# mLSTM state of a hybrid layer: the normalisers through the vector tile and one transpose, the sample state's load behind the last prompt chunk

## The chip, the cores and the metric

The kernel runs on one core of one Trainium2 chip. A core has a matrix engine (TensorE, PE in the profile; PEld is its weight load), a vector engine (VectorE, DVE), an activation engine (ScalarE, ACT), a general engine (GpSimd, POOL) and a queue engine (SyncE, SP) that issues DMA transfers. Each engine runs its own instructions in order; semaphores order them between engines. The metric is the device time of one execution in microseconds (us), the median of several runs.

## The reference

One layer of a streaming encoder, for 1024 prompt tokens without history and 64 sample tokens that continue a stored state. All arrays are float32, the model width is 1024.

```python
z = x @ w_in                      # conv GLU, q/k/v/o heads, gates, two merge gates
# branch A: GLU -> causal depthwise conv (31 taps) -> LayerNorm -> swish -> w_a_out
# branch B: mLSTM, 4 heads of 256; per chunk, with carried (C0, n0, m0):
num = einsum(s, v) + w_inter * einsum(q, C0)
den = sum(s)       + w_inter * einsum(q, n0)
h   = num / maximum(abs(den), exp(-m))
C1  = decay * C0 + einsum(w_end, k, v)
n1  = decay * n0 + einsum(w_end, k)
# head norm, output gate, w_b_out; merge; w_out; LayerNorm; feed-forward; LayerNorm
```

The matrix memory C is 256 x 256 for each head, the normaliser n has 256 numbers for each head. The prompt starts from zeros, the sample from `state_C`, `state_n` and `state_m`. Outputs are the tokens of both streams and, for both, the last 30 rows of the convolution, C, n and m.

## The kernel before

Activations stand feature-major in three chunks of tokens (384, 384 and 320). Every matrix product is done in three passes of rounded high and low parts (`mm3`, L325 to L330: high by high, low by high, high by low). A *unit* (L317) takes one piece of a weight matrix, 1024 x 128: for each of the three chunks of tokens it makes one product of 24 matmuls on PE, hands the result to its own `post` function, and calls `slot` (L119). The weight pieces are loaded two ahead on SP (`wload`, L1105) and split one ahead (`wsplit`, L1111), the high part on ACT, the low part on DVE (`split`, L332).

Beside the units run background generators, which `slot` moves on by hand: one step of the mLSTM of the current head, steps of the depthwise convolution, and one step of a third queue. The convolution's steps are paid from a credit: a slot adds 1.0 where an mLSTM step was done and 1.7 where none was, and each step of the convolution costs 1.0 (L119 to L124). What is left of a generator when a stage ends is drained at once (`drain`, L115). The order that a function writes down is not quite the order on an engine: the framework plans each engine's instructions anew within what their data allow, except where `pin` keeps them in program order. Each tile's buffer is reused when its last readers are done.

At the start, `start_x` (L174) loads and transposes x, then loads 31 rows of the convolution's weights and six rows of vectors into the tile `vp` (L181 to L184) and the convolution's cache into `cp` (L185). Eight transposes on PE turn `vp` into `vecs`, one column for each row and feature (L187 to L190), eight more turn `cp` into `cacheT`. The gates' small weights, bias and `state_m` are loaded next (L219 to L223), and a first product on PE with them is L238.

For each of the four heads, eight units make k, q, v and the output gate o; behind the first o unit the generator `mlstm(h)` (L419) is queued. It walks through nine chunks of 128 tokens: chunks 0 to 7 are the prompt, chunk 8 holds the 64 sample tokens. A chunk takes two steps:

- First half, L451 to L478: the scores k by q and the transposed k on PE, then on ACT and DVE the weighted scores `sm`, split into `smh` and `sml`, and the weighted k, `kwh` and `kwl`.
- Second half, L479 to L520: on PE the scores by v (the first is pinned and waits for `smh`), q by the carried state (`Ch`, `Cl`), and k by v for the new state; DVE makes the new C (L499) and the denominator's terms, POOL two small operations of the norm (L516, L517).

The state tile C is 128 x 2 x 258 with two buffers. Its column 256 holds n, because v has a column of ones there; column 257 is a pad. Its split (`csplit`, L433) makes `Ch` and `Cl`. In chunk 8 the carried state comes from memory: a C tile, its last columns zeroed on POOL (L455), the load of `state_C` (L456, 256 KB) and the load of `state_n` (L457, 1 KB: two numbers into column 256 of each partition), then the split. At the end of chunks 7 and 8 the new state is stored, C by L503 and its n column by L504. All these transfers are issued on SP, in the order L503, L504, L456, L457 at the turn from chunk 7 to chunk 8.

Behind the last head, `close_proj` (L615) drains the mLSTM and the convolution. Then `open_bra` (L651) splits the gated result into the next operand, and units of `w_b_out` begin while the first norm `ln_a` (L730) loads the convolution's output.

Of the kernel before, what the change touches and what calls it, by code (L numbers as in the profile page):

```python
# [9 lines left out]
F32 = mybir.dt.float32  # L10
F32R = mybir.dt.float32r
AF = mybir.ActivationFunctionType
# [9 lines left out]
P = 128  # L22
KT = D // P
NH = 4
HD = 256
CW = 31
CB = CW - 1
# [8 lines left out]
MASKED = -1.0e38  # L36
R_BDW, R_AG, R_AB, R_HN, R_G1, R_B1 = 31, 32, 33, 34, 35, 36
NV = 37

# [10 lines left out]
def hybrid_layer(ctx, tc, x_prompt, x_sample, cache_conv, state_C, state_n, state_m, w_in, b_gate,  # L50
# [3 lines left out]
    nc = tc.nc  # L54
    V, S, G, TE = nc.vector, nc.scalar, nc.gpsimd, nc.tensor
# [8 lines left out]
    const = pool("const")  # L64
# [4 lines left out]
    small = pool("small", 4)  # L69
# [14 lines left out]
    def mtile():  # L84
        return pools["psm"].tile([P, 512], F32, tag="m", name="m")
# [29 lines left out]
    def drain(kind):  # L115
        while step(kind):
            pass
# [7 lines left out]

# [1 line left out]
    ident = const.tile([P, P], F32, name="ident")  # L127
    make_identity(nc, ident)
    vecs = const.tile([P, KT, NV], F32, name="vecs")
# [10 lines left out]
    bgb = const.tile([P, 8], F32, name="bgb")  # L140
    smc = const.tile([P, 1], F32, name="smc")

    proj = ExitStack()

# [1 line left out]
    XH, XL = [], []  # L146
# [27 lines left out]
    def start_x():  # L174
        for i in range(3):
            trans_x(i, xt0[i])
            if i == 1:
                wsplit(0, True)
        for i in range(3, NT):
            trans_x(i, load_x(i))  # L180
        vp = xp.tile([NV, D], F32, tag="x", name="vp")  # L181
        nc.sync.dma_start(vp[0:CW, :], w_dw[0])
        for r, src in ((R_BDW, b_dw), (R_AG, ln_a_g), (R_AB, ln_a_b), (R_HN, hn_g), (R_G1, ln1_g), (R_B1, ln1_b)):
            nc.sync.dma_start(vp[r:r + 1, :], src[0:1, :])  # L184
        cp = xp.tile([CB, D], F32, tag="x", name="cp")  # L185
        nc.sync.dma_start(cp, cache_conv[0, 0])
        ps = mtile()  # L187
        for k in range(KT):
            TE.transpose(ps[:, k * NV:(k + 1) * NV], vp[:, k * P:(k + 1) * P], ident[:NV, :NV])
        V.tensor_copy(vecs, ps[:, :KT * NV].rearrange("p (k v) -> p k v", k=KT))  # L190
        ps = mtile()
        for k in range(KT):
            TE.transpose(ps[:, k * CB:(k + 1) * CB], cp[:, k * P:(k + 1) * P], ident[:CB, :CB])
        V.tensor_copy(cacheT, ps[:, :KT * CB].rearrange("p (k v) -> p k v", k=KT))

    N(start_x)

# [1 line left out]
    def gates():  # L199
# [106 lines left out]

# [1 line left out]
    early, later = [], []  # L308
# [38 lines left out]

# [1 line left out]
    G32 = []  # L349
# [69 lines left out]
    def mlstm(h):  # L419
        ml = pools["ml"]  # L420
        kf, qf, vh, vl, dt = HT["k"], HT["q"], HT["vh"], HT["vl"], HT["dt"]
        W = HD + 2
# [24 lines left out]

        C = Ch = Cl = back = None
        nxt = prep(0)
        for c in range(NT):  # L450
            n, o = tile_len(c), c * P  # L451
            qs, ks = nxt
            if c == 8:
                C = ml.tile([P, 2, W], F32, tag="C", name="C", bufs=2)
                G.memset(C[:, :, HD + 1:], 0.0)  # L455
                nc.sync.dma_start(C[:, :, :HD], state_C[0, 0, h].rearrange("(j p) v -> p j v", p=P))  # L456
                nc.sync.dma_start(C[:, :, HD:HD + 1], state_n[0, 0, h].rearrange("(j p o) -> p j o", p=P, o=1))  # L457
                Ch, Cl = csplit(C)
            pS = mtile()
            for j in range(2):  # L460
                a = TE.matmul(pS[:, :2 * P], ks[:, j, 0, :], qs[:, j].rearrange("p e t -> p (e t)"), start=j == 0, stop=False)
# [38 lines left out]
            C = Cn  # L500
            if c >= 7:
                Cd, nd = (C_prompt, n_prompt) if c == 7 else (C_sample, n_sample)
                nc.sync.dma_start(Cd[0, 0, h].rearrange("(j p) v -> p j v", p=P), C[:, :, :HD])  # L503
                nc.sync.dma_start(nd[0, 0, h].rearrange("(j p o) -> p j o", p=P, o=1), C[:, :, HD:HD + 1])  # L504
            else:
                Ch, Cl = csplit(C)
# [14 lines left out]
            back = (c, n, isb)  # L521
# [93 lines left out]
    def close_proj():  # L615
        drain("mlstm")
        drain("conv")
        proj.close()

    N(close_proj)  # L620

# [1 line left out]
    def set_operand(srcs, pad=False):  # L623
# [22 lines left out]

# [1 line left out]
    A32, MB = [], []  # L648
# [117 lines left out]

# [1 line left out]
    wos = ExitStack()  # L768
# [27 lines left out]

# [1 line left out]
    X1H, X1L, Y2 = [], [], []  # L798
# [48 lines left out]

# [1 line left out]
    stage[0] = 1  # L849
# [160 lines left out]

# [1 line left out]
    HID = {}  # L1012
# [86 lines left out]

# [1 line left out]
    pieces = [j for j in jobs if j[0] is not None]  # L1101
# [70 lines left out]
```

## Time and profile before

| | us |
|---|---|
| median of 3 runs (lowest, highest) | 2013.27 (2013.09, 2013.63) |
| span of the profiled execution | 2012.8 |
| PE busy | 1943.4 (97% of the span) |
| DVE busy | 1426.8 (71%) |
| ACT busy | 648.7 (32%) |
| POOL busy | 126.3 (6%) |

The profile is of one execution. Its span runs from the first to the last instruction; the runs' median is of other executions and lies 0.5 us above it. The mean granted clock of PE is 0.984 of full speed. The chain that ended last, followed back from the end, is 80% PE, 11% DVE, 4% DMA, 2% waiting for nothing that is shown, 2% ACT and 1% POOL.

How to read the rows that follow. A row of the timeline has the start and the length in us, the engine, the line, the operation, output<-inputs and shape; in brackets stands how long the engine was idle before it and who ended that. A row of the waits has the waiting instruction, whom it waited for, the total in us, the number of times and the longest. A row of the windows has the stretch, its length, the busy time and instructions of PE, PEld, DVE, ACT and POOL, the granted clock of PE, the share of the DMA engines and GB/s. A row of the chain has the start, the length and what it was. A row of the groups has the busy time, the mean in ns of one, and the idle time before them.

### The profile page before, as it was taken

What the parts mean: (1) busy time and instruction counts of PE and PEld (TensorE: products, weight loads), DVE (VectorE), ACT (ScalarE), POOL (GpSimd) and SP (SyncE); (2) the same over time, 40 slices, a digit from 0 to 9 for tenths busy, and PEclk for the clock granted to TensorE, in tenths of its full rate; (3) what the DMA queues carried; (4) which work ended last, traced back from release to release, by engine and by line L of the source; (5) the groups of instructions that cost most, each with busy time, mean ns of one, the idle gap of its engine ahead of it and who ended that gap; (6) DMA issues with size and microseconds to landing.
All of it is one profiled execution on the core that took longest, in us unless ns stands there. A gap on an engine that the chain in (4) does not pass through costs nothing.

```text
span 2012.8 us, 30485 instructions
## 1 busy us (share of the span) xinstructions
PE 1943.4 (97%) x12395; PEld 1917.8 (95%) x12395; DVE 1426.8 (71%) x2717; ACT 648.7 (32%) x1209; POOL 126.3 (6%) x220
## 2 busy tenths in 40 slices
PE   8999899998999899989999998999999999999996
PEld 7999899998999899989999998999999999999995
DVE  4957776786678677868885557877686858677647
ACT  4323222333233323323342204524233332414232
POOL 1112210001000100000000000000000000000005
PEclk9999999999999999989999999999999999999998
DMA  4122321122112221225325310111111111111212
GB/s 148 44 78 67 85 70 43 54 67 47 56 41 63 62 63 37 64 66 172 116 82 154 116 40 21 32 53 43 53 42 54 43 43 53 43 53 43 74 42 79
DMA packets 174974, 131.06 MB, mean 65 GB/s; under 512 B 11518, under 2 KB 169694, under 8 KB 174833
## 3 DMA queue, kind: packets, MB, share of 16 engines
q1 hardware_dynamic: 174833, 129.11, 21.8%
q8 instruction: 97, 1.59, 0.3%
q14 instruction: 44, 0.36, 0.1%
HBM read 104.39 MB, written 24.63 MB: 64 GB/s over the span
## 4 chain that ended last, share of the span: by engine, by line
PE 80%; DVE 11%; DMA 4%; issue 2%; ACT 2%; POOL 1%; SPq 0%; POOLq 0%; ACTq 0%; DVEq 0%
PE g L326 25%; PE g L329 25%; PE g L330 25%; DMA C<-in_state_n_dram 2%; DVE s L668 2%; DVE acc L563 1%; PE m L326 1%; PE m L330 1%; PE m L329 1%; DVE o L1091 1%; DVE wl L337 1%; DVE ln L640 0%; DVE a L689 0%; DVE y L689 0%; DVE C L499 0%
## 5 line engine op out<-in xcount | busy, mean ns | idle before, releaser
L326 PE MATMUL g<-xh,wh 128*128 128x384 f32 (+1 forms) x1920 | 636.0, 331 | 0.0
L329 PE MATMUL g<-xl,wh 128*128 128x384 f32 (+1 forms) x1920 | 630.1, 328 | 0.0
L330 PE MATMUL g<-xh,wl 128*128 128x384 f32 (+1 forms) x1920 | 629.6, 328 | 0.0
L326 PEld LDWEIGHTS g<-xh,wh 128*128 128x128 f32 x1920 | 363.1, 189 | 0.4 <-ACT xh L334 0.2
L329 PEld LDWEIGHTS g<-xl,wh 128*128 128x128 f32 x1920 | 363.0, 189 | 0.3
L330 PEld LDWEIGHTS g<-xh,wl 128*128 128x128 f32 x1920 | 362.6, 189 | 0.1
L563 DVE SCALAR_TENSOR_TENSOR acc<-glu,vecs,acc 128x1118 f32<-128x1118 f32 x240 | 332.8, 1387 | 3.9
L334 ACT ACTIVATE wh<-wr 128x1024 fp32r<-128x1024 f32 (+1 forms) x168 | 166.1, 989 | 429.1 <-PE g L329 356.0
L337 DVE TENSOR_TENSOR wl<-wr,wh 128x1024 fp32r<-128x1024 f32 (+1 forms) x168 | 191.4, 1139 | 106.8 <-ACT wh L334 104.2
L326 PE MATMUL g<-x1h,wh 128*128 128x384 f32 (+1 forms) x768 | 253.1, 330 | 0.0
L329 PE MATMUL g<-x1l,wh 128*128 128x384 f32 (+1 forms) x768 | 252.8, 329 | 0.0
L330 PE MATMUL g<-x1h,wl 128*128 128x384 f32 (+1 forms) x768 | 252.6, 329 | 0.0
L329 PE MATMUL g<-hvl,wh 128*128 128x272 f32 x784 | 223.5, 288 | 0.0
L330 PE MATMUL g<-hvh,wl 128*128 128x272 f32 x784 | 221.5, 288 | 0.0
L326 PE MATMUL g<-hvh,wh 128*128 128x272 f32 x784 | 221.1, 289 | 0.1
L967 DVE TENSOR_TENSOR y<-g,y 128x272 f32<-128x272 f32 (+1 forms) x540 | 157.3, 341 | 26.8 <-PE g L330 25.1
L326 PEld LDWEIGHTS g<-hvh,wh 128*128 128x128 f32 x784 | 145.9, 189 | 1.7 <-DVE y L967 1.4
L329 PEld LDWEIGHTS g<-hvl,wh 128*128 128x128 f32 x784 | 147.4, 188 | 0.1
L330 PEld LDWEIGHTS g<-hvh,wl 128*128 128x128 f32 x784 | 146.4, 188 | 0.0
L330 PEld LDWEIGHTS g<-x1h,wl 128*128 128x128 f32 x768 | 144.8, 188 | 0.0
L329 PEld LDWEIGHTS g<-x1l,wh 128*128 128x128 f32 x768 | 144.7, 188 | 0.1
L326 PEld LDWEIGHTS g<-x1h,wh 128*128 128x128 f32 x768 | 144.5, 188 | 0.1
(267 smaller groups left out, 2440.9 us busy)
## 6 DMA issues: line engine op xcount, KB each, us to landing
wr<-in_w_in_dram SPq DMA_DIRECT2D x64, 512.0 KB
wr<-in_w_ff_dram SPq DMA_DIRECT2D x64, 512.0 KB
x<-in_x_prompt_dram SPq DMA_DIRECT2D x8, 512.0 KB
dwT<-acc SPq DMA_DIRECT2D x8, 512.0 KB
wr<-in_w_b_out_dram SPq DMA_DIRECT2D x8, 512.0 KB
wr<-in_w_a_out_dram SPq DMA_DIRECT2D x8, 512.0 KB
wr<-in_w_out_dram SPq DMA_DIRECT2D x8, 512.0 KB
out_dram<-o SPq DMA_DIRECT2D x16, 256.0 KB
```

The lines of the kernel that those rows point to most:

```text
L326: first = TE.matmul(out, lh, rh, start=start, stop=False, skip_group_check=more)
L329: TE.matmul(out, lh, rl, start=False, stop=False, skip_group_check=more)
L330: TE.matmul(out, ll, rh, start=False, stop=stop, skip_group_check=more)
L334: a = S.activation(hi, src, AF.Copy)
L337: V.tensor_tensor(lo, src, hi.bitcast(F32), ALU.subtract)
L563: V.scalar_tensor_tensor(acc, glu[:, j:j + AC], vecs[:, c, j:j + 1], acc, ALU.mult, ALU.add))
L668: V.tensor_reduce(out[:, :n], t[:, :, :n].rearrange("p k t -> p t k"), AX.X, ALU.add)
L967: V.tensor_tensor(y, ps[:, pslc], y, ALU.add)
L1091: V.tensor_tensor(o[:n, hs], o[:n, hs], pools["g2"][:n, hs], ALU.mult)
```

## The change

`state_n` comes in as one more row of `vp` (1024 numbers, one DMA of 4 KB), so that it stands as one more column of `vecs`. The new state tile for chunk 8, `C0`, is made at the end of chunk 7's second half: the load of `state_C` is issued there, ahead of the store of C, and POOL zeroes the last columns and copies n's column from `vecs`. Chunk 8 begins with one more `yield` and then splits `C0`. The stores of n's column are replaced by a copy on POOL into a small tile `nout`; after the last head one transpose on PE, one copy on ACT and two stores, of eight rows of 128 numbers each, send all of it out. Comment lines that were also changed are left out.

```diff
-R_BDW, R_AG, R_AB, R_HN, R_G1, R_B1 = 31, 32, 33, 34, 35, 36
-NV = 37
+R_BDW, R_AG, R_AB, R_HN, R_G1, R_B1, R_SN = 31, 32, 33, 34, 35, 36, 37
+NV = 38
...
     smc = const.tile([P, 1], F32, name="smc")
+    nout = const.tile([P, 2, KT], F32, name="nout")
...
             nc.sync.dma_start(vp[r:r + 1, :], src[0:1, :])
+        nc.sync.dma_start(vp[R_SN:R_SN + 1, :], state_n[0, 0].rearrange("h k -> (h k)")[None, :])
         cp = xp.tile([CB, D], F32, tag="x", name="cp")
...
-        C = Ch = Cl = back = None
+        C = Ch = Cl = back = C0 = None
...
             if c == 8:
-                C = ml.tile([P, 2, W], F32, tag="C", name="C", bufs=2)
-                G.memset(C[:, :, HD + 1:], 0.0)
-                nc.sync.dma_start(C[:, :, :HD], state_C[0, 0, h].rearrange("(j p) v -> p j v", p=P))
-                nc.sync.dma_start(C[:, :, HD:HD + 1], state_n[0, 0, h].rearrange("(j p o) -> p j o", p=P, o=1))
+                yield
+                C = C0
                 Ch, Cl = csplit(C)
...
             if c >= 7:
-                Cd, nd = (C_prompt, n_prompt) if c == 7 else (C_sample, n_sample)
-                nc.sync.dma_start(Cd[0, 0, h].rearrange("(j p) v -> p j v", p=P), C[:, :, :HD])
-                nc.sync.dma_start(nd[0, 0, h].rearrange("(j p o) -> p j o", p=P, o=1), C[:, :, HD:HD + 1])
+                if c == 7:
+                    C0 = ml.tile([P, 2, W], F32, tag="C", name="C", bufs=2)
+                    nc.sync.dma_start(C0[:, :, :HD], state_C[0, 0, h].rearrange("(j p) v -> p j v", p=P))
+                    G.memset(C0[:, :, HD + 1:], 0.0)
+                    G.tensor_copy(C0[:, :, HD:HD + 1], vecs[:, 2 * h:2 * h + 2, R_SN:R_SN + 1])
+                nc.sync.dma_start((C_prompt if c == 7 else C_sample)[0, 0, h].rearrange("(j p) v -> p j v", p=P), C[:, :, :HD])
+                G.tensor_copy(nout[:, c - 7, 2 * h:2 * h + 2, None], C[:, :, HD:HD + 1])
...
     def close_proj():
         drain("mlstm")
+        ps = mtile()
+        TE.transpose(ps[:2 * KT, :P], nout.rearrange("p a k -> p (a k)"), ident)
+        nt = small.tile([CB, 2 * P], F32, tag="cb", name="nt", bufs=1)
+        S.activation(nt[:2 * KT, :P], ps[:2 * KT, :P], AF.Copy)
+        for a, dst in ((0, n_prompt), (1, n_sample)):
+            nc.sync.dma_start(dst[0, 0].rearrange("h (j p) -> (h j) p", p=P), nt[a * KT:(a + 1) * KT, :P])
         drain("conv")
         proj.close()
```

## The prediction, made before the changed kernel had run

> **What bounds the kernel now.** I read the page first, then the totals of waits, then the timeline around the longest of them. The page says that the matrix engine (PE) is the bound nearly everywhere, and that one DMA stands on the chain that ended last:
>
> ```profile
> span 2012.8 us, 30485 instructions
> PE 1943.4 (97%) x12395; PEld 1917.8 (95%) x12395; DVE 1426.8 (71%) x2717; ACT 648.7 (32%) x1209; POOL 126.3 (6%) x220
> ...
> PE g L326 25%; PE g L329 25%; PE g L330 25%; DMA C<-in_state_n_dram 2%; DVE s L668 2%; DVE acc L563 1%; PE m L326 1%; PE m L330 1%; PE m L329 1%; DVE o L1091 1%; DVE wl L337 1%; DVE ln L640 0%; DVE a L689 0%; DVE y L689 0%; DVE C L499 0%
> ```
>
> PE is idle for 2012.8 - 1943.4 = 69.4 us in all. Two per cent of the span is the landing of state_n, a 1 KB load. The totals of waits (total, times, longest) say what that load holds:
>
> ```profile
> PE m L326 <- ACT smh L334: 27.2, 6, 7.3
> ACT Ch L334 <- DMA C<-in_state_n_dram: 35.5, 4, 9.6
> DVE Cl L337 <- ACT Ch L334: 33.7, 5, 9.4
> ```
>
> The four waits of ACT are chunk 8 of the four heads: ACT, in strict order, stands at the split of the loaded state (Ch) and behind it waits smh, which PE needs. PE's first product after the wait, in the four heads:
>
> ```profile
> 246.05 0.58 PE L326 MATMUL m<-vh,smh 128*128 128x258 f32 x1 [6.50 <-ACT smh L334]
> 461.52 0.58 PE L326 MATMUL m<-vh,smh 128*128 128x258 f32 x1 [5.85 <-ACT smh L334]
> 674.06 0.58 PE L326 MATMUL m<-vh,smh 128*128 128x258 f32 x1 [6.51 <-ACT smh L334]
> 886.89 0.58 PE L326 MATMUL m<-vh,smh 128*128 128x258 f32 x1 [7.28 <-ACT smh L334]
> ```
>
> 6.50 + 5.85 + 6.51 + 7.28 = 26.1 us of PE idle time, over a third of the 69.4. There is a second loss that no wait shows. The busy time in stretches of 6 us from each restart (the column ahead of the last two is the granted clock):
>
> ```profile
> 246.05:252.05 6.00, 6.00 (x26) 5.77 (x27) 5.76 (x15) 1.69 (x3) 2.49 (x1) 0.59 0.21 58
> 461.52:467.52 6.00, 6.00 (x27) 5.77 (x28) 5.76 (x15) 1.69 (x3) 2.28 (x1) 0.63 0.24 62
> 674.06:680.06 6.00, 6.00 (x29) 5.76 (x30) 5.76 (x15) 1.70 (x3) 2.20 (x1) 0.70 0.22 59
> 886.89:892.89 6.00, 6.00 (x23) 5.76 (x24) 5.76 (x15) 1.69 (x3) 0.12 (x1) 0.52 0.22 61
> ```
>
> After each gap PE runs part of the 6 us at a lower clock: 6 x (0.41 + 0.37 + 0.30 + 0.48) = 9.4 us of work lost. Together the gaps cost 26.1 + 9.4 = 35.5 us.
>
> **Why the load is late.** Head 0, SP's queue and ACT:
>
> ```profile
> 232.44 0.39 SPq L503 DMA_DIRECT2D out_dram<-C  x1
> 232.88 0.46 SPq L504 DMA_DIRECT2D out_dram<-C  x1
> 233.39 0.49 SPq L456 DMA_DIRECT2D C<-in_state_C_dram  x1
> 233.93 0.47 SPq L457 DMA_DIRECT2D C<-in_state_n_dram  x1
> ...
> 235.85 0.47 ACT L339 ACTIVATE kwh<-m,cols 128x256 fp32r<-128x256 f32 x1
> 245.16 0.63 ACT L334 ACTIVATE Ch<-C 128x516 fp32r<-128x516 f32 x1 [8.84 <-DMA C<-in_state_n_dram]
> ```
>
> The loads were already issued as soon as chunk 7's state was made; they were not late in program order. ACT is free at 236.32, and the last load lands at about 245.1, 11.2 us after its issue. What the transfers did meanwhile (the last two columns are the DMA engines' share and GB/s):
>
> ```profile
> 232.50:235.00 2.50, 2.50 (x16) 2.50 (x15) 1.47 (x8) 0.00 (x0) 1.31 (x5) 1.00 0.86 220
> ...
> 237.00:239.00 2.00, 2.00 (x15) 2.00 (x15) 1.27 (x4) 0.00 (x0) 0.00 (x0) 1.00 0.28 22
> 239.00:241.00 2.00, 0.55 (x5) 0.30 (x3) 0.00 (x0) 0.00 (x0) 0.00 (x0) 1.00 0.12 16
> 241.00:243.00 2.00, 0.00 (x0) 0.00 (x0) 0.00 (x0) 0.00 (x0) 0.00 (x0) 1.00 0.05 11
> ```
>
> At 220 GB/s the 256 KB of state_C would take 1.2 us; from 237 to 243 the rate is 11 to 22. I read that as the two transfers of n, which move 256 single elements of 4 bytes each (one element a partition, twice): the store L504 ahead of state_C, and the load L457 behind it.
>
> **Part 1: the load.** In the changed kernel the load of state_C is the first DMA behind chunk 7, ahead of C_prompt's store; both n transfers are gone from this place, and n's column of the state is copied by POOL from the vector tile. Issue moves from 233.39 to about 232.44, where L503 stood (both wait for the same release, chunk 7's last use of the other C buffer). Its time to landing alone is not in the trace. Bounds: two rows of the chain of waits, a 17 KB transfer and the slowest of the four landings now:
>
> ```profile
> 75.17 1.83 DMA fa<-fc
> ...
> 874.20 11.70 DMA C<-in_state_n_dram
> ```
>
> So not under 1.83 and not over 11.7 us. I take 1.83 + 1.2 = 3.0 us, near the lower end, since the row that differs, the element transfers, is what leaves. It lands at about 235.5, before ACT was free even in the old order.
>
> **Part 2: the extra yield.** Chunk 8's first half moves one slot later. A slot is one product of 24 matmuls; two neighbouring evictions give its length:
>
> ```profile
> 254.71 0.49 ACT L538 ACTIVATE sg<-g 128x384 f32<-128x384 f32 x1 [5.55 <-PE g L330]
> 258.87 0.49 ACT L538 ACTIVATE sg<-g 128x384 f32<-128x384 f32 x1 [3.67 <-PE g L330]
> ```
>
> 258.87 - 254.71 = 4.2 us. ACT then meets Ch at about 236.3 + 4.2 = 240.5, 8.1 us after the issue. Any landing faster than 8.1 us costs nothing: the two edits each cover most of the wait, and together they have 5 us to spare. So all 35.5 us should go. What is late next in that place is smh itself, as in other chunks: 27.2 - 26.1 = 1.1 us in two waits outside these four, so 0.6 us apiece; I add one such wait, +0.6 (from 0 to 4 x 0.6 = 2.4).
>
> The Trainium skill, page "TensorE: Matmul & The Clock Gate", section on the HAM clock gate, says that a restart after an idle window runs at half rate for about one window of 3.4 us. By that the clock's part would be 4 x 1.7 = 6.8 us and the sum 2.6 us higher; the granted clock above shows longer slow stretches, so I keep 9.4.
>
> The yield has a price in the schedule. Each head's generator has one step more; from its start to the next head's drain there are 24 slots and it now takes 20 full steps, so nothing is drained without cover. A slot with mLSTM work credits the convolution with 1.0 instead of 1.7 steps. Counting all 192 slots through, the convolution ends exactly at the last slot before, and with one step left over after. What such a step costs (last row), and what DVE waits for right after the close:
>
> ```profile
> 949.09 5.80 DVE L668 TENSOR_REDUCE s<-a 128x384 f32<-128x1536 f32 x2 [0.53 <-DMA a<-dwT]
> 959.72 0.56 DVE L753 TENSOR_TENSOR mb<-g,sb 128x384 f32<-128x384 f32 x1 [1.21 <-PE g L330]
> 963.23 0.49 DVE L753 TENSOR_TENSOR mb<-g,sb 128x320 f32<-128x320 f32 x1 [2.96 <-PE g L330]
> ...
> L563 DVE SCALAR_TENSOR_TENSOR acc<-glu,vecs,acc 128x1118 f32<-128x1118 f32 x240 | 332.8, 1387 | 3.9
> ```
>
> The step is 1.39 us of DVE, ahead of the operand split and of the first norm's load. DVE idles 1.21 + 2.96 = 4.2 us behind PE there, so the 1.4 us is hidden; without that cover it costs 1.4, and up to 4 x 0.7 x 1.39 = 3.9 if all lost credit came due at once.
>
> **Part 3: n in and out.** In: a seventh row load before cp's at the start. The order there:
>
> ```profile
> 17.31 0.30 SPq L182 DMA_DIRECT2D vp<-in_w_dw_dram  x1
> ...
> 19.60 0.32 SPq L186 DMA_DIRECT2D cp<-in_cache_conv_dram  x1
> 25.44 0.40 SPq L1109 DMA_DIRECT2D wr<-in_w_in_dram  x1
> ...
> SPq L1109 <- DMA vp<-in_w_dw_dram: 5.5, 1, 5.5
> ...
> 30.74 0.44 PE L238 MATMUL g<-xh,wg 128*128 128x384 f32 x1 [1.66 <-DVE wg L232]
> ```
>
> The weight load L1109 has nothing to do with vp, yet it waited for w_dw's landing. It is the eighth DMA behind it, which looks like eight completion counters used in turn. With a row more, cp becomes the eighth and waits until 25.44 in its place; weight, gate and bias loads follow 25.44 - 25.04 = 0.4 us later (an issue and its gap, taken from the 0.40 of the row), and L238, which waits on them with PE idle, starts 0.4 later: +0.4 us. cp's own transposes stand on PE ahead of L238; with a landing of 3 us, 28.4, they are in time. Bounds: 0 (if the counters are not what holds it) to 2.8 (if cp takes as long as w_dw, 25.44 - 17.31 = 8.1 us: 33.5 - 30.74). The vector tile's transposes and its copy grow by one column in 38: nothing.
>
> Out: rows nearest to what is new there, and in the chunks:
>
> ```profile
> L553 ACT ACTIVATE cb<-m 30x256 f32<-30x256 f32 x8 | 2.9, 360 | 2.3 <-PE m L551 2.3
> L550 PE MATMUL m<-ident,glu 128*30 128x128 f32 x8 | 2.2, 272 | 0.0
> L516 POOL TENSOR_SCALAR st<-st 128x1 f32<-128x1 f32 (+1 forms) x36 | 8.2, 229 | 500.3 <-DVE st L515 477.7 <-issue 22.6
> ```
>
> Eight n stores leave SP for eight POOL copies of two elements a partition, and four more POOL copies fill the state's column: 12 x 0.23 = 2.8 us of an engine that is 6% busy. They wait for DVE's update of the state (L499); behind them on POOL stands L516, which needs a later DVE result (L515) anyway. Ch now waits for the column's copy too, with the 8.1 us above as its cover. So nothing; on the path of chunk 8 the copy would be 0.23 a head.
>
> At the close one transpose is +0.3 us on PE. The ACT copy behind it (0.36) stands ahead of the operand's splits; its cover is ACT's 32% load. The two stores wait for that copy and hold SP for about 0.9 us, with the loads of the gate spill and of the first norm queued behind; they are hidden by the same 4.2 us of DVE idle time, which then carries 1.4 + 0.4 + 0.9.
>
> **The sum**, against the profiled span: 2012.8 - 26.1 - 9.4 + 0.6 + 0.4 + 0.3 = 1978.6. The median of the runs, 2013.27, lies 0.5 above the span; I carry that over: **1979 us**.
>
> **The rivals.**
>
> *The load stays as late as now* (8 in 100): what holds it is not the element transfers but the bulk ahead of it, and only the yield helps. Then it lands 232.44 + 11.7 = 244.1, ACT waits 244.1 - 240.5 = 3.6 instead of 8.84, and PE 6.5 - 5.2 = 1.3 a head, too short a gap for the clock: 1979 + 5 = 1984. For it: state_C's own landing is not shown. Against: 220 GB/s just before.
>
> *The close shows the lost credit* (4 in 100): the last convolution step and the two stores delay the first norm by more than the 4.2 us: up to +4, 1983.
>
> *The gaps were catching-up time* (5 in 100): DVE stood up to 9.4 us in each gap; without it, DVE's backlog returns as waits in the next chunks and half the gain is lost: 2013 - 17 = 1996. Against: DVE is at 71% on the whole and after each restart is busy 5.76 of 6 us for one stretch only.
>
> *Slower* (3 in 100): the order on ACT is not the program's (Ch stands behind kwh now, though the code has it first). If Ch is put right behind chunk 7 and the load still takes 11.7 us, ACT stands from 232.4 on, and sm and kwh, now done in the gap, come after it: about 2 us more PE wait a head, 2013 + 8 = 2021. It decides only where the landing is over 8.1 us and Ch moves ahead of kwh.
>
> **How the numbers follow.** My forecast has 80 in 100. Its own bounds: all small costs nil, 1977.8, and I allow 1 to 2 us more because the n stores of chunk 8 leave the queues too; residual waits of 2.4 and a start of 2.8 instead of 0.6 and 0.4, 1983.3. The range takes in the first two rivals and, for the first, some of these small costs on top: 1976 to 1987. The last two are left out. No change within 0.2% (4 us, what a measurement can tell here) has 2 in 100, slower 3, faster 95.
>
> **What would show it.** Right: no wait of ACT's Ch on a DMA, PE's waits on smh about 1 to 3 us in all, a granted clock of 1.00 through chunk 8 of every head, PE idle near 34 us, and L238 at about 31.1. Wrong: a new releaser ahead of Ch (POOL's column copy or the load), a lower clock at those places, or more waits of PE on sh (L701, L715) after 940.

## The result, and the profile after

| | before | after |
|---|---|---|
| median of 4 runs each, us | 2013.45 | 1988.67 |
| lowest to highest, us | 2013.09 to 2015.0 | 1988.33 to 1988.86 |
| span of the profiled execution, us | 2012.8 | 1986.8 |
| mean granted clock of PE | 0.984 | 0.991 |

The ratio is 0.9881, with a 95% interval of 0.9867 to 0.9895: 24.8 us less. I had forecast 1979, with a range of 1976 to 1987. The direction was right; the gain is a good quarter smaller than the 34 us that I had worked out, and the time lies 1.7 us outside the range. In the changed kernel `Ch` and `smh` are made at L336, the first product of a chunk's second half is L328, the transposes of the gated output are L445, and POOL's and DVE's steps of the norm are L520 to L523. The totals of the page, and the waits that answer to those of the prediction (total, times, longest):

```profile
span 1986.8 us, 30495 instructions
PE 1938.1 (98%) x12396; PEld 1914.4 (96%) x12396; DVE 1425.0 (72%) x2717; ACT 642.8 (32%) x1206; POOL 124.9 (6%) x232
```

```profile
ACT Ch L336 <- DMA C<-in_state_C_dram: 12.4, 3, 4.3
PE m L445 <- DVE isb L523: 7.0, 3, 2.5
...
PE m L328 <- ACT smh L336: 1.1, 2, 0.6
```

The 26.1 us of PE's waits on `smh` in chunk 8 are gone to the last tenth: 27.2 have become the 1.1 that lay elsewhere before. ACT still waits for the load of state_C in three heads, for up to 4.3 us, but PE does not wait for ACT there. Head 1, SP and ACT:

```profile
440.83 0.38 SPq L504 DMA_DIRECT2D C<-in_state_C_dram  x1
...
443.91 0.64 ACT L336 ACTIVATE Ch<-C 128x516 fp32r<-128x516 f32 x1 [3.98 <-DMA C<-in_state_C_dram]
```

The load is there 3.1 us after its issue. In place of the gaps stands a wait that the sum did not have: 7.0 us of PE, in heads 0, 1 and 2, before the transposes of the gated output, for the result of the norm of chunk 8. Before, one such wait of 1.8 us was there:

```profile
PE m L443 <- DVE isb L519: 1.8, 1, 1.8
```

Who comes late is seen on the chain of waits of the changed kernel, followed through head 1 (start, length, what):

```profile
454.35 1.37 POOL dt L386
...
456.50 6.83 issue
463.33 1.11 POOL st L520
...
464.99 0.60 POOL st L521
465.79 1.33 DVE isb L523
467.17 0.33 PE m L445 x2
```

POOL's timeline of the same stretch shows where the chain's part before that comes from:

```profile
448.23 0.20 POOL L377 MEMSET k<- 128x128 f32 x1 [5.05 <-PE m L467]
454.35 1.36 POOL L386 PARTITION_BROADCAST dt<-negM  x1 [5.91 <-issue]
...
463.33 1.11 POOL L520 TENSOR_SCALAR st<-st 64x1 f32<-64x1 f32 x1 [6.90 <-issue]
```

At this place POOL prepares the next head. Ahead of the partition broadcast of the decay row (L386, in `head_start`) it does nothing that the profile shows for 5.91 us, and behind it, before the small addition of the norm, again for 6.90 us. What the trace has there are entries on POOL's queue under the same two lines (count, durations in ns, first and last start):

```profile
L386 POOLq MODIFY_POOL_CONFIG  x8: 7/10/12, 43.8 to 656.5; - x8
...
L520 POOLq MODIFY_POOL_CONFIG  x4: 4/4/4, 456.5 to 664.4; - x4
```

In head 1 they stand at 448.6 and 456.5, at the start of each empty stretch. There is also one semaphore entry under L386, at 450.6, when DVE's last reader of the old `dt` is done (L473, 450.24 + 0.28); the broadcast starts 3.7 us after it, so that wait is not what ends the stretch. The Trainium skill, page "GPSIMD Engine Reference", section "Instruction dispatch", says that the first call of a newly loaded POOL routine pays about 6 us for bringing its code in, with no visible instruction. The 5.91 us agree with that, the 6.90 are a microsecond longer; that code is what comes in here, no row shows. From the memset that opens this path to the end of L521 it takes 465.58 - 448.23 = 17.35 us of a single in-order queue, and the norm of chunk 8 stands at the end of it.

The kernel before had the same path, and there it was longer, 475.18 - 451.99 = 23.19 us from the memset to the end of L517:

```profile
464.09 2.28 POOL L384 PARTITION_BROADCAST dt<-negM  x1 [11.90 <-DVE g L446]
473.79 0.25 POOL L516 TENSOR_SCALAR st<-st 64x1 f32<-64x1 f32 x1 [7.41 <-issue]
...
474.59 0.59 POOL L517 TENSOR_TENSOR st<-st,mhalf 64x1 f32<-64x1 f32 x1
...
475.40 0.40 DVE L519 TENSOR_SCALAR isb<-isb,st 64x256 f32<-64x256 f32 x1
...
476.34 0.33 PE L443 MATMUL m<-ident,isb 64*128 64x64 f32 x2
```

It did not show, because PE stood in the gap of 5.85 us and then ran at half clock during it. From PE's products of chunk 8 to the transposes of the gated output it was 476.34 - 461.52 = 14.82 us before. After, with PE's first such product at

```profile
452.31 0.36 PE L328 MATMUL m<-vh,smh 128*128 128x258 f32 x1
```

it is 467.17 - 452.31 = 14.86 us: as long, only that before this time was work, a part of it at a low clock, and now it ends in a wait. (Two steps at the end of the path are longer in this execution: 1.11 us for 0.25 on POOL, 1.33 for 0.40 on DVE.) The granted clock of the changed kernel (third column from the right), in chunk 8 of head 1 and behind the new wait:

```profile
448.00:450.00 2.00, 2.00 (x14) 2.00 (x13) 1.50 (x3) 1.33 (x4) 0.20 (x1) 1.00 0.20 68
...
465.00:467.00 2.00, 0.00 (x0) 0.00 (x0) 1.36 (x2) 0.00 (x0) 1.90 (x3) 1.00 0.69 156
467.00:469.00 2.00, 1.83 (x9) 1.76 (x10) 2.00 (x5) 1.99 (x7) 0.00 (x0) 0.81 0.35 106
469.00:471.00 2.00, 2.00 (x8) 2.00 (x7) 2.00 (x3) 0.75 (x3) 0.00 (x0) 0.50 0.00 0
471.00:473.00 2.00, 2.00 (x11) 2.00 (x11) 1.97 (x2) 0.00 (x0) 0.00 (x0) 0.84 0.00 0
```

In chunk 8 it is 1.00. After the new wait 2 x (0.19 + 0.50 + 0.16) = 1.7 us of work are lost; head 2 loses 2 x (0.39 + 0.47) = 1.7 in the same way (0.61 and 0.53 in two windows from 676), head 0 nothing. Head 0 of the kernel before had lost 1.7 us behind its one wait there:

```profile
264.00:266.00 2.00, 2.00 (x11) 2.00 (x10) 2.00 (x4) 1.44 (x3) 2.00 (x2) 0.65 0.00 0
266.00:268.00 2.00, 2.00 (x8) 2.00 (x7) 2.00 (x2) 1.99 (x4) 1.16 (x1) 0.50 0.00 1
```

The start is the second difference. The first gate product begins 31.35 - 30.74 = 0.6 us later, and runs at half clock, which it did not before:

```profile
31.35 0.69 PE L240 MATMUL g<-xh,wg 128*128 128x384 f32 x1 [1.23 <-DVE wg L234]
```

```profile
30.00:32.00 2.00, 0.77 (x4) 0.66 (x4) 1.07 (x6) 1.20 (x2) 0.00 (x0) 0.83 0.36 76
32.00:34.00 2.00, 2.00 (x8) 2.00 (x7) 0.00 (x0) 0.34 (x1) 0.00 (x0) 0.50 0.62 187
34.00:36.00 2.00, 2.00 (x11) 2.00 (x11) 0.00 (x1) 0.00 (x0) 0.00 (x0) 0.81 0.00 0
```

That is 2 x (0.17 + 0.50 + 0.19) = 1.7 us more. Put together, between the two profiled executions: gaps -26.1, clock behind them -9.4, start +0.6 + 1.7, waits on the norm 7.0 - 1.8 = +5.2, clock behind those +1.7 + 1.7 - 1.7 = +1.7. The sum is -26.3; the spans differ by 26.0.

### The profile page after: what moved, and what is told of

Same layout as the page of the kernel before. It is cut to its first block, busy times and chain, and to the rows that moved or that the text cites. A ratio compares the mean times of both kernels' runs of the same rounds, so it can differ in the third digit from the quotient of the medians.

```text
span 1986.8 us, 30495 instructions
## 1 busy us (share of the span) xinstructions
PE 1938.1 (98%) x12396; PEld 1914.4 (96%) x12396; DVE 1425.0 (72%) x2717; ACT 642.8 (32%) x1206; POOL 124.9 (6%) x232
## 4 chain that ended last, share of the span: by engine, by line
PE 83%; DVE 9%; issue 3%; ACT 1%; POOL 1%; DMA 1%; SPq 0%; POOLq 0%; ACTq 0%; DVEq 0%
PE g L328 26%; PE g L331 26%; PE g L332 26%; DVE s L678 2%; PE m L328 1%; PE m L332 1%; PE m L331 1%; DVE o L1101 1%; DVE acc L567 1%; DVE ln L650 0%; DVE a L699 0%; DVE y L699 0%; PE m L461 0%; DMA x<-in_x_prompt_dram 0%; PE m L1061 0%
## 5 line engine op out<-in xcount | busy, mean ns | idle before, releaser
L328 PE MATMUL g<-xh,wh 128*128 128x384 f32 (+1 forms) x1920 | 637.7, 332 | 0.0
L328 PEld LDWEIGHTS g<-xh,wh 128*128 128x128 f32 x1920 | 363.7, 189 | 0.4 <-ACT xh L336 0.2
L336 ACT ACTIVATE wh<-wr 128x1024 fp32r<-128x1024 f32 (+1 forms) x168 | 166.0, 988 | 445.9 <-PE g L331 355.7
L328 PE MATMUL g<-x1h,wh 128*128 128x384 f32 (+1 forms) x768 | 253.4, 331 | 0.0
L328 PE MATMUL g<-hvh,wh 128*128 128x272 f32 x784 | 221.4, 290 | 0.0
L328 PEld LDWEIGHTS g<-hvh,wh 128*128 128x128 f32 x784 | 146.0, 189 | 1.7 <-DVE y L977 1.3
L328 PEld LDWEIGHTS g<-x1h,wh 128*128 128x128 f32 x768 | 144.6, 188 | 0.1
```

The source lines that it names most:

```text
L328: first = TE.matmul(out, lh, rh, start=start, stop=False, skip_group_check=more)
L336: a = S.activation(hi, src, AF.Copy)
```

## The experiments

My theory after the result: what comes late next is POOL's queue at the change of heads, about 13 us of it without an instruction, and the new operations on POOL and the extra yield have little to do with it. The rivals: the new POOL copies or the extra yield made the norm late. Two further questions stood open from the prediction: whether the element transfers of n had really held the load, and which part of the change was worth what. Runs e1 to e4 were made side by side, then e5 to e8, then e9 to e11. Each ratio is against runs of the kernel before on the same chip beside them; the changed kernel's own four runs are from another time, so a few us between it and a run here rest on the profiles as well as on the medians.

**e1: POOL's broadcast replaced in heads 1 to 3.**

```diff
+        nc.sync.dma_start(nmD, negM[0:P:32, :])
...
-        G.partition_broadcast(dt.rearrange("p c t -> p (c t)")[:, :T], negM[32 * h:32 * h + 1, :])
+        if h == 0:
+            G.partition_broadcast(dt.rearrange("p c t -> p (c t)")[:, :T], negM[32 * h:32 * h + 1, :])
+        else:
+            nc.sync.dma_start(dt.rearrange("p c t -> p (c t)")[:, :T], nmD[h:h + 1, :].partition_broadcast(P))
```

> The changed kernel, with the next head's row of decay terms spread over the partitions by a DMA from a DRAM row (heads 1 to 3) instead of POOL's partition broadcast; head 0 keeps POOL's. Theory (POOL's path is what is late next): behind the gaps that went, POOL stands about 6 us with no instruction of the page ahead of the broadcast and about 7 us behind it, so that chunk 8's norm and PE's transpose of the gated output come 2.5 us late. Then PE's three waits of the transpose on the norm's result (7.0 us in all) go, and so do the stretches of half clock behind them in heads 1 and 2 (2.8 us): 1988.7 - 9.8 = about 1979, bounds 1977 to 1982. Rival (the new POOL copies of n, or the extra yield, delay the norm by themselves): the three waits stay at 2 us or more, 1987 to 1990. Rival (the waits go, but the clock drops are a matter of where the clock's window falls): 1982.

Measured: 1978.22 us (1977.46 to 1980.62), ratio 0.9829 (0.9815 to 0.9844). PE's waits on the norm, and the windows at the place in head 1 that answers to the ones above:

```profile
PE m L450 <- DVE isb L528: 2.6, 3, 1.6
```

```profile
454.00:456.00 2.00, 1.64 (x10) 1.31 (x8) 0.45 (x2) 1.98 (x6) 1.39 (x4) 1.00 0.01 2
456.00:458.00 2.00, 1.84 (x13) 1.78 (x14) 2.00 (x5) 1.95 (x4) 0.00 (x0) 1.00 0.00 0
```

7.0 us have become 2.6, of which 1.6 is head 0, and the clock stays at 1.00. The entries `MODIFY_POOL_CONFIG` are gone from the norm's line (L525 here), and so is the empty stretch ahead of it: in head 1 the step starts right behind the copy ahead of it. All POOL copies and the yield are still in. The theory's 1979 was met; the rival that blamed the copies or the yield alone is out. Of the 10.4 us between this run and the changed kernel, 4.4 are these waits and 3.4 the clock behind them. About 2 are the start, which ran at full clock in this execution; no row ties that to the edit.

**e2: without the extra yield.**

```diff
             if c == 8:
-                yield
                 C = C0
```

> The changed kernel without the extra yield ahead of chunk 8. The load lands about 3.1 us after its issue and ACT reaches the split 3.9 us after it, so the load should still be covered. Theory (POOL's path): chunk 8's products and POOL's queue move together, so the three waits of the gated output's transpose on the norm stay at about 2 to 4 us each and the time is 1988.7 within 3. Rival (the extra yield is what made the norm late): the waits go, 1979 to 1982. Rival (the yield carries the cover of the load, as my sum had it in part): ACT's split waits for the load by 1 us or more a head and PE for smh.

Measured: 1983.93 us (1981.66 to 1984.68), ratio 0.9854 (0.9839 to 0.9868). Neither side was right as it stood: the waits fell to 4.0 us in all, most of it in head 0. In head 1 POOL's queue reads

```profile
443.68 0.21 POOL L377 MEMSET k<- 128x128 f32 x1 [1.52 <-PE m L466]
449.72 1.37 POOL L386 PARTITION_BROADCAST dt<-negM  x1 [5.83 <-DVE isb L488]
...
458.13 0.25 POOL L519 TENSOR_SCALAR st<-st 64x1 f32<-64x1 f32 x1 [6.79 <-issue]
...
458.93 0.59 POOL L520 TENSOR_TENSOR st<-st,mhalf 64x1 f32<-64x1 f32 x1
```

The two empty stretches are the same. But the first small step of the norm now stands ahead of the memsets of vh and takes 0.25 us instead of 1.11, and the path is 459.52 - 443.68 = 15.84 us, 1.5 less than the 17.35 above. With the yield, the compiled order on POOL puts the memsets ahead. So the yield does cost something, and the order on POOL would account for it; the theory had that wrong. Whether it has a price of its own is tested by e5.

**e3: only the handling of n.** state_C's load is back where it was, behind the store, and there is no yield.

```diff
             if c == 8:
+                C = ml.tile([P, 2, W], F32, tag="C", name="C", bufs=2)
+                nc.sync.dma_start(C[:, :, :HD], state_C[0, 0, h].rearrange("(j p) v -> p j v", p=P))
+                G.memset(C[:, :, HD + 1:], 0.0)
+                G.tensor_copy(C[:, :, HD:HD + 1], vecs[:, 2 * h:2 * h + 2, R_SN:R_SN + 1])
-                yield
-                C = C0
```

> The changed kernel's handling of n (a row of the vector tile, out through one transpose) alone; state_C's load stays where it was, behind chunk 7's store at the start of chunk 8, and there is no extra yield. If the element transfers of n were what kept the landing at 11 us, the load lands about 3 to 4 us after its issue at the same place, ACT is free 2.9 us after that issue, PE's gaps shrink from 6.5 us to under 1 and the time is 1988 to 1992. If the bulk store ahead of it held it (the rival of the prediction), the gaps stay at 5 us or more and the time is over 2005.

Measured: 1983.04 us (1981.74 to 1984.01), ratio 0.9849 (0.9833 to 0.9865): less than the 1988 expected. ACT's waits for the load are 0.5 us in all, and PE's on the norm 2.7, with the broadcast still on POOL. The handling of n does it alone; moving the load and yielding add nothing to it, and in the changed kernel they cost some 5 us.

**e4: only the earlier load and the yield.** Both loads stand ahead of both stores; n still moves element by element.

```diff
+                if c == 7:
+                    C0 = ml.tile([P, 2, W], F32, tag="C", name="C", bufs=2)
+                    nc.sync.dma_start(C0[:, :, :HD], state_C[0, 0, h].rearrange("(j p) v -> p j v", p=P))
+                    nc.sync.dma_start(C0[:, :, HD:HD + 1], state_n[0, 0, h].rearrange("(j p o) -> p j o", p=P, o=1))
...
+                yield
```

> The kernel before with the loads of state_C and state_n, both as they were, issued behind chunk 7 and ahead of the two stores, and the extra yield; n still moves by element transfers of 4 bytes. The moved load starts 1 us earlier, has one element transfer fewer ahead of it, and the yield gives it 4 us more: if one element transfer takes about 7 us by itself, state_n lands about 8 us after its issue against a cover of 7 to 8 us, ACT waits 0 to 1.5 us a head, and the time is 1985 to 1990 (the start stays as before, 2.3 us less than in the changed kernel). If element transfers hold the load wherever it is issued, it lands 11 us after and PE still waits 2 to 3 us a head: 1995 to 2003.

Measured: 1999.78 us (1996.52 to 2001.38), ratio 0.9932 (0.9917 to 0.9947). The time lies in the second case, but not for its reason. SP and ACT in head 1:

```profile
443.16 0.46 SPq L503 DMA_DIRECT2D C<-in_state_n_dram  x1
...
445.93 0.64 ACT L334 ACTIVATE Ch<-C 128x516 fp32r<-128x516 f32 x1 [4.13 <-DMA C<-in_state_n_dram]
```

Ahead of the stores, the load of n's single elements was there 2.8 us after its issue, and PE waits for `smh` 1.0 us in all. The loss is at the norm:

```profile
PE m L443 <- DVE isb L522: 18.0, 3, 7.8
```

```profile
458.62 1.37 POOL L384 PARTITION_BROADCAST dt<-negM  x1 [8.33 <-DVE st L518]
...
469.71 0.25 POOL L519 TENSOR_SCALAR st<-st 64x1 f32<-64x1 f32 x1 [9.24 <-issue]
```

POOL's empty stretches are 8.33 and 9.24 us instead of 5.91 and 6.90. An element store of n was issued ahead of each, at 444.19 and at 457.56. So a store of single elements is the suspect, perhaps in a second way too: POOL's empty stretches are longer with it. Runs e7 and e8 take the two directions apart.

**e5: e1 without the yield.** The edits of e1 and e2 together.

> The changed kernel with the decay row of heads 1 to 3 by DMA and without the extra yield. Without the yield alone the time fell to 1983.9, with the DMA alone to 1978.2. If the yield hurt only by the order that POOL's instructions got (two memsets ahead of the second 6.9 us stretch without an instruction), it has nothing left to hurt in heads 1 to 3 once that stretch is gone: 1976 to 1979, as with the yield. If the yield has a price of its own (the convolution's lost credit, or later stores), the two gains add: 1978.2 - 4.7 = about 1973.5.

Measured: 1980.30 us (1979.27 to 1981.63), ratio 0.9835 (0.9815 to 0.9855), against 0.9829 with the yield. That is a microsecond over the bounds, and nowhere near the 1973.5 of gains that add: once POOL's path is short, no price of the yield can be told within the two intervals. This fits a price that lies in POOL's order.

**e6: the broadcast by DMA in the kernel before.** The edit of e1, on the kernel before.

> The kernel before with the decay row of heads 1 to 3 by DMA instead of POOL's broadcast, nothing else. Theory: in the kernel before, the state's late load made PE stop anyway and POOL's path lay in that stop's shadow; only head 0's wait of 1.8 us on the norm and the half clock behind it can go: 2013.2 - 3 = about 2010, bounds 2009 to 2014 (the DMA's own element or row transfers may cost as much). Rival (POOL's path costs the same in both kernels, and the changed kernel only shows it): 2003.

Measured: 2013.59 us (2008.95 to 2016.38), ratio 1.0004 (0.9992 to 1.0015). The same edit that is worth 10 us in the changed kernel is worth nothing here: PE's waits on `smh` stay.

```profile
PE m L328 <- ACT smh L336: 28.7, 6, 7.6
```

So POOL's path lay in the shadow of the late state, as the theory said; the 3 us that I had allowed for head 0 did not come, within an interval of about 2.3 us each way.

**e7: only the loads of n through the vector tile.** The stores of n stay.

```diff
-                nc.sync.dma_start(C[:, :, HD:HD + 1], state_n[0, 0, h].rearrange("(j p o) -> p j o", p=P, o=1))
+                G.tensor_copy(C[:, :, HD:HD + 1], vecs[:, 2 * h:2 * h + 2, R_SN:R_SN + 1])
```

> The kernel before with only the loads of n through the vector tile's row; the stores of n stay element by element, state_C's load stays behind them. With the load of n issued ahead of the stores it was out of the way 2.7 us after its issue (the order of SP's issues and ACT's start), so a store of single elements is the suspect, not the load. If the store of n holds the load of state_C behind it: ACT still waits 7 to 8 us a head, 2006 to 2013. If the load of n was the slow one (the prediction's reading put it on both): ACT's wait falls by half or more, 1992 to 2000.

Measured: 2020.61 us (2017.28 to 2025.23), ratio 1.0037 (1.0027 to 1.0048). Head 1:

```profile
449.30 0.49 SPq L457 DMA_DIRECT2D C<-in_state_C_dram  x1
...
460.80 0.63 ACT L335 ACTIVATE Ch<-C 128x516 fp32r<-128x516 f32 x1 [8.42 <-DMA C<-in_state_C_dram]
```

With no element load at all, the load of state_C behind the element store comes 11.5 us after its issue. This half of the handling of n gives nothing. That it is even slower than before by 0.4%, I had not expected. The profiled execution's span is 3.6 us longer than the one before: its waits on `smh` are shorter (24.4 us for 27.2), but PE is busy for 1950.9 us instead of 1943.4. Why, stays open.

**e8: only the stores of n through the transpose.** The loads stay, element load behind the load of state_C.

```diff
-                nc.sync.dma_start(nd[0, 0, h].rearrange("(j p o) -> p j o", p=P, o=1), C[:, :, HD:HD + 1])
+                G.tensor_copy(nout[:, c - 7, 2 * h:2 * h + 2, None], C[:, :, HD:HD + 1])
```

> The kernel before with only the stores of n through the columns of one tile and one transpose at the end; the loads of state_C and of n stay where and as they were. If the store of n is the slow one: both loads land about 3 to 4 us after their issue, ACT waits 0 to 1.5 us a head, PE's gaps go and POOL's stretches are about 6 and 7 us: 1980 to 1985. If the load of n holds it: ACT waits 4 us or more a head and the time is 1993 to 2005.

Measured: 1989.73 us (1987.74 to 1991.39), ratio 0.9882 (0.9865 to 0.9900). Head 1:

```profile
444.81 0.46 SPq L457 DMA_DIRECT2D C<-in_state_C_dram  x1
445.32 0.49 SPq L458 DMA_DIRECT2D C<-in_state_n_dram  x1
...
448.25 0.63 ACT L335 ACTIVATE Ch<-C 128x516 fp32r<-128x516 f32 x1
```

ACT reaches the split 2.9 us after the issue of the element load and does not wait. The stores of n alone were what kept the load; this one line and its transpose bring 22 us (2011.82 beside it). POOL's rows at the same place:

```profile
454.95 1.36 POOL L385 PARTITION_BROADCAST dt<-negM  x1 [6.40 <-DVE C L500]
...
463.68 0.25 POOL L516 TENSOR_SCALAR st<-st 64x1 f32<-64x1 f32 x1 [7.12 <-issue]
```

This run differs from the kernel before in the stores of n alone, and the stretch ahead of the broadcast fell from 11.90 to 6.40 us; in e7, with the stores, it is 11.66. The second one hardly changes (7.41, here 7.12, in e7 7.55). The time is some 5 us over what I expected; the profiled execution has waits of 4.3 us on the norm, 2.4 of them in head 0 with a half clock behind it.

**e9: the row of n behind cp.**

```diff
-        nc.sync.dma_start(vp[R_SN:R_SN + 1, :], state_n[0, 0].rearrange("h k -> (h k)")[None, :])
         cp = xp.tile([CB, D], F32, tag="x", name="cp")
         nc.sync.dma_start(cp, cache_conv[0, 0])
+        nc.sync.dma_start(vp[R_SN:R_SN + 1, :], state_n[0, 0].rearrange("h k -> (h k)")[None, :])
```

> The changed kernel with the row load of n issued behind the load of cp instead of ahead of it, so that cp is again the seventh DMA behind w_dw's. Theory (the start's delay is cp's issue, held until w_dw's landing): cp is issued at about 20 us instead of 25.45, the first gate product starts about 0.6 us earlier (30.7 instead of 31.35), and the time is 1988.7 - 0.6 = about 1988 (bounds 1986 to 1989). If the rest of the 2.3 us that the start lost (the other order of the transposes of x, the half clock at 32 to 34 us) hangs on cp as well, 1986.4.

Measured: 1988.07 us (1984.92 to 1991.44), ratio 0.9866 (0.9848 to 0.9883). cp is issued at 20.28 instead of 25.45, as meant, but the first gate product starts at 31.40 all the same, and at half clock. Another kernel with the changed kernel's own start (e2) began it at 30.21 at full clock, and e4, which has the start of the kernel before, ran at clocks of 0.58 and 0.56 from 30 to 34 us. So the start's loss looks like scatter between executions, not the row's work; no effect of the row's place can be measured. The waits on the norm are 7.0 us here again, and POOL's path in head 1 is 468.44 - 451.09 = 17.35 us, as in the changed kernel, though its first small step takes 0.28 us.

**e10 and e11: what is left.** e10 is e1 and e9 together; e11 is the same without the yield and with state_C's load in its old place.

> The changed kernel with the decay row of heads 1 to 3 by DMA and the row load of n behind cp's. The two act in different places, so the gains add: 1978.2 - 0.6 = about 1977.5 (bounds 1976 to 1979).

> The same, but state_C's load in its old place behind chunk 7's store and no extra yield: only the handling of n and of the decay row is left of all changes. If neither the moved load nor the yield is worth anything once the element stores are gone, the time is that of the run beside it within 1.5 us, 1976 to 1980. If the earlier load still hides something, it is slower by 2 us or more.

Measured: 1977.65 us (1977.02 to 1978.40), ratio 0.9819 (0.9805 to 0.9834), and 1979.35 us (1977.53 to 1982.05), ratio 0.9829 (0.9813 to 0.9845). The two can't be told apart. Both beat the kernel before and the changed one: n as a row and a transpose, and the decay row by DMA, are enough for all of it, 34 us in e11.

## Why the prediction was right or wrong

**The gaps: right.** All four went, with 26.1 us, and the clock behind them with 9.4; the clock in chunk 8 is 1.00, the load no longer ends a wait of PE. The residual 0.6 for smh did not come: still 1.1 us in two waits. One sign was added up wrongly: "PE idle near 34 us" takes the 9.4 us off the idle time too, though they are work at a lower clock. By the sum's own terms it is 69.4 - 26.1 + 1.0, about 44; measured are 1986.8 - 1938.1 = 48.7, the waits on the norm among them.

**The reason for the late load: half right.** The landing alone, put at 3.0 us from a far row, was 3.1 in head 1. I put the late landing on the two element transfers of n, store and load alike. e7 and e8 show that it was the store: with the element load alone left ACT does not wait, with the element store alone it waits 8.4 us. The rival that the bulk ahead of the load held it is out by e3, where the load stands behind the same bulk store and costs ACT 0.5 us in all.

**The two covers: wrong, without harm to PE.** I wrote that the moved load and the yield each cover most of the wait, with ACT at Ch 8.1 us after the issue. The compiled order puts Ch ahead of chunk 8's sm and kwh: ACT stands at it and takes it when it lands, after 3.1 us, so the sign "no wait of ACT's Ch on a DMA" failed. The yield's slot then lies behind Ch, and smh still comes in time. e3 shows that n alone was enough, and e2 that without the yield the changed kernel is about 5 us faster.

**The step that failed** is "What is late next in that place is smh itself", priced at 0.6 us, and with it the words on POOL: "behind them on POOL stands L516, which needs a later DVE result (L515) anyway". Late next was the norm at the end of POOL's path: 5.2 us more of waits and 1.7 of clock, 6.9 us where the sum had 0.6. The span came out 8.2 us above the 1978.6 of the sum; most of the rest is the start.

I looked at what the twelve copies cost, 2.8 us of an engine that is 6% busy, and not at what POOL's queue held at that place. The busy share hid it, for the two stretches have no instruction. The rows were in the trace of before: the broadcast with 11.90 us of idle time ahead of it, and L516 with 7.41 us that the view calls issue. The view puts the 11.90 down to DVE's L446, which ended at 464.01, just ahead; but the broadcast neither reads nor overwrites what L446 handles. Its own semaphore entry stands at 453.0, when the last reader of `dt` was done. L516 did not wait for L515 either, which ended at 467.32, 6.5 us ahead of it. L517 at the end of that path was done at 474.59 + 0.59 = 475.18, and PE came to L443 at 476.34, only 1.2 us later, and 0.5 us after the DVE step that it needs (475.40 + 0.40), although it had stood for 5.85 us and lost 6 x 0.37 = 2.2 us of work to the clock. Without that delay of 8.1 us PE was bound to be there first, with POOL's path as it was. What no row of before showed is that the path itself shrinks when the element stores go, from 23.19 to 17.35 us; 8.1 - 0.5 - 5.8 leaves a wait of 1.8 us, and 2.3 were measured.

It takes the broadcast and the yield together. Without the broadcast (e1) the waits are 2.6 us, without the yield 4.0 (e2) or 2.7 (e3, where the load is in its old place too), with both 7.0. That e1's 1978.2 us lies so near the 1979 forecast is in part luck: some 2 us of it are a start that ran well.

**The start: mis-sized, and mostly scatter.** The sum had +0.4; between the profiles it was 0.6 and 1.7 of clock. The mechanism that I named is there (cp is issued at 25.45, behind w_dw's landing), but e9 took it away and nothing changed. By e2, e4 and e9 it is scatter of the first 36 us; what sets it stays open.

**The rivals.** That the gaps had been catching-up time came nearest, in kind: work of another engine was done in their shadow, and came back as a wait. It named DVE in the next chunks, and 17 us; it was POOL in chunk 8, and about 7 us with its clock. Of the slower case one half occurred, Ch ahead of kwh on ACT; the fast landing made it harmless. The late load of the first rival did not occur; its clause that a stop of 1.3 us is too short for the clock stands on no row, and the stop of 1.8 us in head 0 of the kernel before was followed by clocks of 0.65 and 0.50. No cost of the close can be made out: PE's waits on sh and sl, over all the norms, are 14.9 us, 13.7 before, and no run takes that apart. My range reached to cases with a load that stays late, and not to the possibility that a second path ends within a few us of the one removed.

**The clock.** The prediction kept 9.4 us by rows where its estimate from the page "TensorE: Matmul & The Clock Gate" of the Trainium skill was 6.8. That page's section on the HAM clock gate has the clock fall after an idle window of about 3.4 us, and calls the window free-running. Here stops of 2.3 us cost 1.7 us each in heads 1 and 2, and one of 2.5 us in head 0 nothing. So stops shorter than that window did bring the clock down, and a rule by the length of the stop alone does not fit these three. Whether it matters where in such a window a stop falls, no run here shows.

## What to carry to other kernels

Before counting a stall as gain, follow every other queue through the same place and note when each would be done without the stall: the smallest of those distances is what can be won until the next one shows, and an engine with a busy share of 6% can be the one. Idle time that a view calls "issue", or gives to a releaser that the instruction does not need, is a cost like an instruction's and belongs on that list. And when a transfer of 1 KB is late, look at what stands ahead of it in its queue before moving it; here it was a store of the same 1 KB.

## What the runs showed of the hardware

A store of n to memory, 256 runs of 4 bytes, holds what is queued behind it: state_C's load came 11.5 us after its issue behind it (e7), and within 3.4 us without it (e8). A load of the same shape ahead of the stores took 2.8 us (e4). The Trainium skill, page "DMA: Bandwidth & Descriptors", in its specifications, has transfers under 512 bytes done by a read-modify-write; that line does not set the store apart from the load, and no run here shows the mechanism itself.

The element store also lengthens the empty stretch of POOL ahead of the broadcast. In heads 0, 1 and 2 it is 12.18, 11.90 and 12.64 us before and 11.40, 11.66 and 11.44 in e7, both with the stores; 6.02, 6.40 and 6.20 in e8, which lacks them and nothing else. The stretch behind the broadcast is in head 1 7.41 and 7.55 us with the stores, 7.12 without; in e4 it is 9.24. What fills these stretches, and why a store lengthens them, no run here shows.
